# Second layer of a two-layer encoder: how the positional part of the latent heads is rotated and multiplied, and one block of values placed earlier

## The chip, the cores and the metric

One core of a Trainium2 chip runs the whole kernel. The metric is the device time of one execution in microseconds (us); lower is better. The engines that matter are TensorE (PE, matrix products, with its weight loads PEld), VectorE (DVE), ScalarE (ACT), GpSimd (POOL), and SyncE (SP), which issues nearly all DMA transfers. Each engine takes its own instructions in the order in which they were written to its queue.

## The reference, cut to what matters

Two layers; in each, two groups of attention heads read one input projection, and a dense MLP follows. The change touches the second group, multi-head latent attention. The sequence has 256 tokens, and there are 8 latent heads. A head's scores are a sum of a content part (128 features) and a positional part (64 features, rotated by the token's position); the positional key is shared by all heads.

```python
def _rope(x, cos, sin):
    half = x.shape[-1] // 2
    x1, x2 = x[..., :half], x[..., half:]
    out = jnp.concatenate([x1 * cos - x2 * sin, x2 * cos + x1 * sin], axis=-1)
    return out.astype(x.dtype)

# latent attention, per block of queries
s = (jnp.einsum('bhqd,bhkd->bhqk', qn, knt)
     + jnp.einsum('bhqr,bkr->bhqk', qr, k_rope)).astype(jnp.float32) * scale
p = jax.nn.softmax(s, axis=-1)
return jnp.einsum('bhqk,bhkd->bhqd', p.astype(vt.dtype), vt)

# where its inputs come from, in layer l
q = (_rmsnorm(cq, q_norm_g[l]) @ w_uq[l]).reshape(B, S, MLA_HEADS, MLA_NOPE + MLA_ROPE)
q_nope = q[..., :MLA_NOPE]
q_rope = _rope(q[..., MLA_NOPE:], cos[:, :, None, :], sin[:, :, None, :])
kv = (_rmsnorm(ckv, kv_norm_g[l]) @ w_ukv[l]).reshape(B, S, MLA_HEADS, MLA_NOPE + MLA_V)
k_nope, v_m = kv[..., :MLA_NOPE], kv[..., MLA_NOPE:]
k_rope = _rope(kr, cos, sin)
```

All data is float32.

## The kernel before, in words

**Split products.** Most products are not done in fp32. Both operands are split into a high part `hi`, the value rounded to the type fp32r, and a low part `lo`, the rest; then hi x hi, hi x lo and lo x hi are added up in PSUM (`mac`, lines L194, L197 and L198; for values with tokens as rows `tokens_by_k`, L296 to L298). Weights come from memory as fp32 blocks of 128x2048 (1 MB, tile `raw`, 5 buffers), and each half of a block is converted by ACT (`hi`, L151) and DVE (`lo`, L154) into one of 4 buffers each. Some products take fp32 operands as they are: scores, transposes, and the products of probabilities and values. In the trace an fp32 product appears as two records, one of fp32r operands as one.

**Stages of the second layer's attention.** First the projections: the compressed queries `cq`, the compressed keys and values `ckv`, then the queries, keys and the positional key of the input projection. `keys` makes the positional key (`rope_k`). `col` and `probs` make the keys and the probabilities of the 4 differential heads, `turn` transposes those. Then come small up-projections, each of one block of weights: `up_k` (keys of the 8 latent heads, tiles `kn`), `up_q(0)` and `up_q(1)` (content queries, `qn`), `up_r` (positional queries, `qr`) and `up_v` (latent values, `vm`, in banks `pv`). `val(cg, kq)` are 8 blocks of the differential heads' values, 24 products each; the four blocks of a group add up in two PSUM banks (`pv`), which they hold until the fourth has been done.

**A latent head** is three steps from `mla_steps`: `scores` (products into a bank `psm`, one row half of 128 tokens after the other, then a softmax on DVE and ACT), `turn` (a transpose, tile `pt`, copied by ACT to `aT`), and `values` (bank `pom`). The list `mla` holds the steps of all 8 heads staggered: scores of one head, the transpose of the one before, the values of the one before that. Its first six steps stand between the up-projections; the remaining 18 and two steps of the differential heads are handed to `interleave`, which puts them between the blocks of `val`.

**The positional part.** A tile `qr` has 128 rows: 64 features of one head and 64 of the next, for two such pairs. Rotation needs each group of 32 rows exchanged with its neighbour. `rope_q` does that by a product with a permutation matrix (line L1222, bank `pqr`), then three DVE steps with `cos` and `sin` (L1225 to L1227). The key `kr` has two versions, one with the key in rows 0 to 63 and zeros below (set by POOL) and one the other way round, so that a product over all 128 rows picks out one of the two heads (L1319); L1318 is the content product.

**What sets the order.** A scheduler puts each engine's instructions in line by their dependences and by its own estimate of when they become ready; the order of the calls in `layer` breaks ties. PSUM has 8 banks of 2 KB per row. Between the blocks the columns of `w_ada`, the modulation's weights, are loaded (tile `ada`) and summed on DVE (L380), a number per block set by `rate`.

Of the kernel before, what the change touches and what calls it, by code (L numbers as in the profile page):

```python
# [9 lines left out]
F32 = mybir.dt.float32  # L10
F32R = mybir.dt.float32r
I32 = mybir.dt.int32
AF = mybir.ActivationFunctionType
ALU = mybir.AluOpType
AX = mybir.AxisListType

P = 128
T = 256
# [4 lines left out]
HM = 8  # L23
# [78 lines left out]
class Trunk:  # L102
# [764 lines left out]
    def layer(self, l, acc=None):  # L867
        nc, io = self.nc, self.io
        qs = 1.0 / math.sqrt(128.0)
        ms = 1.0 / math.sqrt(192.0)  # L870
# [29 lines left out]
        cq, ckv = [], []  # L900
        kk, qn, kn, qr, vm, a, at, v, o = [], [], [], [], [], [], [], [], []
        self.mo = []

        def keys():
            ps = self.bank("pkr")
            self.tile_cols(ps[:, 0], io["w_kr"][l], h)
            self.kr = self.rope_k(ps[:, 0])

        def col(i, out, scale):
            def f():  # L910
# [7 lines left out]
        def up_k():  # L918
            kn.extend(self.copy(ps, "kn") for ps in self.small(io["w_uk"][l], ckv, 8))
# [2 lines left out]
            qn.extend(self.copy(ps, "qn", ms) for ps in self.small(io["w_uq"][l, b], cq, 4))  # L922

        def up_r():
            raw = [self.copy(ps, "qr", ms) for ps in self.small(io["w_uq"][l, 2], cq, 4)]
            qr.extend(self.rope_q(x) for x in raw)

        def up_v():
            w = self.weights(io["w_uv"][l])
# [5 lines left out]
        def val(cg, kq):  # L935
            def f():
                if kq == 0:
                    self.pv = [self.bank("pv") for _ in range(2)]
                w = self.weights(io["w_dv"][l, cg, kq])
                w = [[z[:, 512 * j : 512 * j + 512] for z in y] for y in w for j in range(2)]  # L940
                self.tokens_by_k(self.pv, w, h[4 * kq : 4 * kq + 4], kq == 0, kq == 3)
                if kq == 3:
                    v.append([self.copy(ps, "v").rearrange("p a b -> p (a b)") for ps in self.pv])
            return f

        def probs(hd):
            return lambda: a.append(self.diff_probs(l, hd, q[hd], kk[hd]))

        def turn(hd):
            return lambda: at.append(self.transposed(a[hd]))  # L950

        av = [self.diff_steps(l, hd, at, v, o) for hd in range(HD)]
        heads = [self.mla_steps(hm, qn, qr, kn, vm) for hm in range(HM)]
        mla = []
        for i in range(HM + 2):
            for s in range(3):
# [9 lines left out]
        kk.append(self.copy(later[0], "k", -1.0))  # L966
        q.append(self.copy(later[1], "q", qs))
        keys()
        order = [(0, kk, -1.0), (2, kk, -1.0), (4, kk, -1.0)]
        for n, (i, dst, scale) in enumerate(order):  # L970
# [4 lines left out]
            col(i + 1, dst, scale)()  # L975
        if l:
            self.rate = RATE_A2
        up_k()
        probs(3)()
        if l == 0:  # L980
# [2 lines left out]
                nc.sync.dma_start(self.xr[:, t], io["x"][t])  # L983
        up_q(0)
        turn(0)()
        up_r()
        turn(1)()
        mla[0]()
        up_v()
# [7 lines left out]
        if l == 0:  # L997
            self.rate = RATE_V
        self.interleave(
            [val(cg, kq) for cg in range(2) for kq in range(4)],  # L1000
            mla[6:] + [av[0][0], av[1][0]],
        )
        if l == 0:
# [9 lines left out]
        o = self.mo + o  # L1013
# [11 lines left out]
        for fb in range(NFB):  # L1025
            hid = []
            done = 12 - 6 * l
            for m in range(0 if fb else done, NK, 2):
                srcs = [io[f"w_m1{l}"][NK * fb + m + j - done] for j in range(2)]
                ps = self.wides(srcs, h)  # L1030
# [197 lines left out]
        return raw  # L1228


    def softmax_parts(self, s, least):

        nc = self.nc
        tot, r = self.s("tot"), self.s("r")
        for t in range(2):
            nc.scalar.activation(
                s[:, t], s[:, t], AF.Exp, bias=least[:, t : t + 1], scale=-1.0, accum_out=tot[:, t : t + 1]
            )
        nc.vector.reciprocal(r, tot)
        return r  # L1240
# [65 lines left out]

        return values, turn

    def mla_steps(self, hm, qn, qr, kn, vm):
        nc = self.nc  # L1310
        st = {}

        def scores():
            ps = self.bank("psm")
            s, mx = self.t("sm"), self.s("mxm")
            for t in range(2):
                c = slice(t * P, (t + 1) * P)
                nc.tensor.matmul(ps[:, t], qn[hm // 2][:, hm % 2, c], kn[hm // 2][:, hm % 2], start=True, stop=False)  # L1318
                nc.tensor.matmul(ps[:, t], qr[hm // 4][:, (hm // 2) % 2, c], self.kr[:, hm % 2], start=False, stop=True)  # L1319
            for t in range(2):  # L1320
                nc.vector.tensor_scalar(s[:, t], ps[:, t], -1.0, None, ALU.mult, ALU.min, accum_out=mx[:, t : t + 1])
            r = self.softmax_parts(s, mx)
            for t in range(2):
                nc.scalar.activation(s[:, t], s[:, t], AF.Copy, scale=r[:, t : t + 1])
            st["s"] = s

        def turn():
            st["t"] = self.transposed(st["s"])

        def values():  # L1330
            if hm % 2 == 0:
                self.pom = self.bank("pom")
            for kt in range(2):
                c = (hm % 4) * P
                v = vm[hm // 4][kt].rearrange("p a b -> p (a b)")
                nc.tensor.matmul(self.pom[:, hm % 2], v[:, c : c + P], st["t"][:, kt], start=kt == 0, stop=kt == 1)
            if hm % 2:
                self.mo += self.split(self.pom, "mo", True)

        return scores, turn, values  # L1340


# [91 lines left out]
```

## Time and profile before

| | |
|---|---|
| median of 3 runs | 2174.59 us (2174.57 to 2177.94) |
| profiled execution, its time | 2174.76 us |
| profiled execution, its span in the trace | 2172.8 us |
| granted TensorE clock, mean | 0.994 |
| second layer's small up-projections start | about 1257 us into the span |
| its last block of values ends | about 1359 us |
| memory read | 589.66 MB, 273 GB/s over the span |

The span is the time from the first to the last instruction in the trace; the device time is some 2 us longer. In the page's rows, "busy" is the time in which an engine has an instruction under way. The chain that ended last is a sequence of pieces of work, each of which released the next; what is not on it costs nothing by itself. A row of a group of instructions reads: line, engine, operation, output<-input, shape, count, then total busy us and mean ns, then the idle time of the engine before it and what ended that. PEclk is the granted clock of TensorE as a share of full speed. A fence of the profile below holds rows word for word; a line of "..." stands for rows left out.

### The profile page before, as it was taken

How to read it: one execution, taken by the hardware profiler on the slowest of the kernel's cores; microseconds unless marked ns; L12 is line 12 of the kernel's file. 1: busy time of each engine (PE TensorE's matmuls, PEld its weight loads, DVE VectorE, ACT ScalarE, POOL GpSimd, SP SyncE). 2: the span in 40 equal slices, each digit the busy share in tenths (PEclk: the TensorE clock that was granted, in tenths of full speed). 3: DMA queues.
4: the chain of work that ended last, by engine and by line, in shares of the span. 5: the costliest groups of instructions: out<-in, count | busy, mean ns of one | idle time of the engine just before them, and what ended most of it. 6: DMA issues, size and time to landing. Idle time of an engine off the chain costs nothing.

```text
span 2172.8 us, 29358 instructions
## 1 busy us (share of the span) xinstructions
PE 2144.7 (99%) x11502; PEld 1863.5 (86%) x11502; DVE 1590.9 (73%) x2117; ACT 1139.8 (52%) x1725; POOL 6.8 (0%) x19
## 2 busy tenths in 40 slices
PE   7999999999999999999999999999999999999998
PEld 6899888898888888888889998888888888888886
DVE  7888888988688988888876876678555555555555
ACT  6555663565455355355454565556535534644643
POOL 0000000000000000000000000000000000000000
PEclk8999999999999999999999999999999999999999
DMA  9988889799888988888967766767655555565552
GB/s 387 423 340 330 320 328 357 290 330 344 314 329 326 352 315 320 321 333 320 336 224 278 253 229 224 290 214 273 233 199 182 200 194 177 192 208 179 194 195 96
DMA packets 87243, 594.76 MB, mean 274 GB/s; under 512 B 9856, under 2 KB 10304, under 8 KB 20288
## 3 DMA queue, kind: packets, MB, share of 16 engines
q1 hardware_dynamic: 85968, 587.08, 73.5%
q0 software_dynamic: 848, 5.28, 0.6%
q8 instruction: 90, 1.47, 0.3%
q10 hardware_dynamic: 288, 0.52, 0.1%
q14 instruction: 49, 0.40, 0.1%
HBM read 589.66 MB, written 3.18 MB: 273 GB/s over the span
## 4 chain that ended last, share of the span: by engine, by line
PE 97%; DVE 2%; DMA 1%; ACT 0%; SPq 0%; issue 0%; ACTq 0%
PE ps L217 19%; PE pr L312 13%; PE pr L311 13%; PE pr L314 13%; PE ps L220 10%; PE pk L260 3%; PE pk L284 2%; PE pk L194 2%; PE pk L198 2%; PE pk L197 2%; PE pv L298 2%; PE pv L296 2%; PE pv L297 2%; PE pk L281 1%; PE ps L198 1%; PE ps L197 1%
## 5 line engine op out<-in xcount | busy, mean ns | idle before, releaser
L154 DVE TENSOR_TENSOR lo<-raw,hi 128x1024 fp32r<-128x1024 f32 (+1 forms) x714 | 836.0, 1194 | 446.2 <-issue 215.5
L151 ACT ACTIVATE hi<-raw 128x1024 fp32r<-128x1024 f32 (+1 forms) x714 | 732.5, 1036 | 694.0 <-PE pr L312 375.9
L380 DVE SCALAR_TENSOR_TENSOR ada<-ada,cond 128x2048 f32<-128x2048 f32 x192 | 438.0, 2285 | 12.0 <-DMA ada<-in_w_ada 11.4
L217 PE MATMUL ps<-h,hi 128*128 128x512 f32 x1856 | 431.5, 390 | 0.0
L217 PEld LDWEIGHTS ps<-h,hi 128*128 128x128 f32 x1856 | 345.2, 188 | 69.4
L311 PE MATMUL pr<-hi,hid 128*128 128x512 f32 x1024 | 398.6, 389 | 0.0
L312 PE MATMUL pr<-hi,hid 128*128 128x512 f32 x1024 | 398.5, 389 | 0.0
L314 PE MATMUL pr<-lo,hid 128*128 128x512 f32 x1024 | 253.5, 389 | 0.0
L220 PEld LDWEIGHTS ps<-h,lo 128*128 128x128 f32 x1856 | 230.3, 192 | 4.5
L220 PE MATMUL ps<-h,lo 128*128 128x256 f32 x1856 | 231.7, 283 | 0.0
L314 PEld LDWEIGHTS pr<-lo,hid 128*128 128x128 f32 x1024 | 192.2, 188 | 39.9
L312 PEld LDWEIGHTS pr<-hi,hid 128*128 128x128 f32 x1024 | 192.3, 188 | 39.7
L311 PEld LDWEIGHTS pr<-hi,hid 128*128 128x128 f32 x1024 | 192.2, 188 | 39.6
L1192 ACT ACTIVATE sum<-ps 128x256 f32<-128x256 f32 x110 | 42.1, 382 | 117.8 <-PE ps L220 117.7
L194 PE MATMUL pk<-h,hi 128*128 128x256 f32 x320 | 90.5, 285 | 0.2 <-ACT h L705 0.2
L198 PE MATMUL pk<-h,lo 128*128 128x256 f32 x320 | 90.5, 283 | 0.0
L197 PE MATMUL pk<-h,hi 128*128 128x256 f32 x320 | 90.5, 283 | 0.0
L260 PE MATMUL pk<-hf,w 128*128 128x256 f32 x384 | 84.1, 379 | 0.5 <-ACT hf L677 0.5
L188 DVE TENSOR_TENSOR hid<-relu,hid 128x256 fp32r<-128x256 f32 x128 | 48.3, 421 | 49.5 <-ACT hid L187 49.5
L260 PEld LDWEIGHTS pk<-hf,w 128*128 128x128 f32 x384 | 72.7, 190 | 10.7 <-ACT hf L677 0.9
L194 PEld LDWEIGHTS pk<-h,hi 128*128 128x128 f32 x320 | 61.1, 192 | 0.6 <-ACT h L705 0.5
L198 PEld LDWEIGHTS pk<-h,lo 128*128 128x128 f32 x320 | 61.3, 192 | 0.2 <-DVE lo L154 0.2
(237 smaller groups left out, 2456.1 us busy)
## 6 DMA issues: line engine op xcount, KB each, us to landing
raw<-in_w_m SPq DMA_DIRECT2D x238, 1024.0 KB, 5.2
ada<-in_w_ada SPq DMA_DIRECT2D x192, 1024.0 KB, 6.5
raw<-in_w_o SPq DMA_DIRECT2D x32, 1024.0 KB, 6.0
raw<-in_w_m SPq DMA_DIRECT2D x24, 768.0 KB, 5.7
raw<-in_w_dv SPq DMA_DIRECT2D x16, 1024.0 KB, 5.5
raw<-in_w_t SPq DMA_DIRECT2D x12, 1024.0 KB, 5.2
w<-in_w_a SPq DMA_DIRECT2D x24, 384.0 KB, 13.5
raw<-in_w_a SPq DMA_DIRECT2D x12, 768.0 KB, 5.4
```

Of the source, the lines that this page charges most:

```text
L151: ins = self.nc.scalar.activation(hi, v, AF.Copy)
L154: ins = self.nc.vector.tensor_tensor(lo, v, hi.bitcast(F32), ALU.subtract)
L194: ins = mm(ps, hi, x[0], start=first, stop=False, skip_group_check=shared)
L197: mm(ps, hi, x[1], start=False, stop=False, skip_group_check=shared)
L198: self.last_mac = mm(ps, lo, x[0], start=False, stop=last, skip_group_check=shared)
L217: mm(ps.rearrange("p a b -> p (a b)"), part(w, k, 0), x[2], start=k == 0, stop=False)
L220: mm(ps[:, 0], part(w, k, 1), x[0], start=False, stop=k == nk - 1)
L260: self.nc.tensor.matmul(ps, v, whole[k], start=first, stop=last, skip_group_check=True)
L311: mm(ps, xh[:, c], part(i, 0), start=kq == 0 and i == 0, stop=False)
L312: mm(ps, xl[:, c], part(i, 0), start=False, stop=False)
L314: self.last_mm = mm(ps, xh[:, c], part(i, 1), start=False, stop=kq == 3 and i == 3)
L380: ins = nc.vector.scalar_tensor_tensor(w, w, 1.0, self.cond, ALU.mult, ALU.mult, accum_out=acc[:, i : i + 1])
```

## The change

It is made in the second layer alone (`l` is 1), but for one detail.

- **Rotation by moved copies.** `rope_q_parts` takes the place of the permutation product: ACT copies the up-projection's bank to `qr` as before, and copies it a second time to `qrr` in four pieces of 32 rows, each to the neighbouring 32 rows. DVE then does the three steps on tiles in SBUF.
- **Split form on 128 rows.** For each head a tile `qrs` is made whose rows hold the high part of its 64 rotated features (a cast on ACT) and, in the other 64 rows, the low part (a subtraction on DVE). The key is split likewise (`rope_k_parts`): its two versions are now the high part and the low part, each repeated in both row halves; the zeros set by POOL go. A head's row half then takes two fp32r products in place of one fp32 product.
- **Order.** `up_r` is called ahead of `up_k` and no longer after the first `turn`; in its place stands the first block of values, `val(0, 0)`. `interleave` gets the remaining 7 blocks for the same 20 steps.
- **In both layers** the second row half of a head now begins with its positional product; in the first layer the products themselves are as before.

```diff
-            self.kr = self.rope_k(ps[:, 0])
+            self.kr = (self.rope_k_parts if l else self.rope_k)(ps[:, 0])
...
         def up_r():
+            if l:
+                qr.extend(self.rope_q_parts(ps, ms) for ps in self.small(io["w_uq"][l, 2], cq, 4))
+                return
             raw = [self.copy(ps, "qr", ms) for ps in self.small(io["w_uq"][l, 2], cq, 4)]
-            qr.extend(self.rope_q(x) for x in raw)
+            qr.extend([self.rope_q(x)] * 2 for x in raw)
...
+        vals = [val(cg, kq) for cg in range(2) for kq in range(4)]
+        if l:
+            up_r()
         up_k()
         probs(3)()
...
         up_q(0)
         turn(0)()
-        up_r()
+        if l == 0:
+            up_r()
+        else:
+            vals.pop(0)()
         turn(1)()
         mla[0]()
...
         self.interleave(
-            [val(cg, kq) for cg in range(2) for kq in range(4)],
+            vals,
             mla[6:] + [av[0][0], av[1][0]],
         )
...
+    def rope_k_parts(self, ps):
+        nc = self.nc
+        t = self.t("krt")
+        for i in range(2):
+            s = slice(64 * i, 64 * i + 64)
+            nc.vector.tensor_tensor(t[s, 0], ps[:64], self.cos[:64], ALU.mult)
+            nc.vector.tensor_tensor(t[s, 1], ps[64:], self.sin[:64], ALU.mult)
+        both = self.t("krb")[:, 0]
+        for i in range(2):
+            s = slice(64 * i, 64 * i + 64)
+            nc.vector.tensor_tensor(both[s], t[s, 0], t[s, 1], ALU.add)
+        out = self.u("kr", F32R)
+        nc.scalar.activation(out[:, 0], both, AF.Copy)
+        nc.vector.tensor_tensor(out[:, 1], both, out[:, 0].bitcast(F32), ALU.subtract)
+        return out
+
+    def rope_q_parts(self, ps, scale):
+        nc = self.nc
+        raw = self.copy(ps, "qr", scale)
+        rot = self.t("qrr")
+        for i in range(4):
+            j = i ^ 1
+            nc.scalar.activation(rot[32 * i : 32 * i + 32], ps[32 * j : 32 * j + 32], AF.Copy, scale=scale)
+        wide = lambda x: x.unsqueeze(1).broadcast_to([P, 2, T])
+        nc.vector.tensor_tensor(rot, rot, wide(self.sin), ALU.mult)
+        nc.vector.tensor_tensor(raw, raw, wide(self.cos), ALU.mult)
+        nc.vector.tensor_tensor(raw, raw, rot, ALU.add)
+        out = []
+        for i in range(2):
+            both = self.u("qrs", F32R)
+            s, o = (slice(64 * j, 64 * j + 64) for j in (i, 1 - i))
+            nc.scalar.activation(both[s], raw[s], AF.Copy)
+            nc.vector.tensor_tensor(both[o], raw[s], both[s].bitcast(F32), ALU.subtract)
+            out.append(both)
+        return out
...
-                nc.tensor.matmul(ps[:, t], qn[hm // 2][:, hm % 2, c], kn[hm // 2][:, hm % 2], start=True, stop=False)
-                nc.tensor.matmul(ps[:, t], qr[hm // 4][:, (hm // 2) % 2, c], self.kr[:, hm % 2], start=False, stop=True)
+                rope = qr[hm // 4][hm % 2][:, (hm // 2) % 2, c]
+                if l:
+                    steps = [(rope, self.kr[:, 0]), (rope, self.kr[:, 1])]
+                else:
+                    steps = [(rope, self.kr[:, hm % 2])]
+                steps.insert(len(steps) * t, (qn[hm // 2][:, hm % 2, c], kn[hm // 2][:, hm % 2]))
+                for i, (w, x) in enumerate(steps):
+                    nc.tensor.matmul(ps[:, t], w, x, start=i == 0, stop=i == len(steps) - 1)
```

How the engines' instructions stand now, at three places of the second layer. A row is a line of the kernel, an operation, its output tile <- its input tiles, and a shape; the numbers behind names tell tiles apart. The changed kernel's lines are its own (L1315 is the transpose, L1372 every product of a head's scores, L1283 the softmax's exponential).

PE, from the end of the up-projection of positional queries to the first latent head's scores, before (`pt` is the transpose of a differential head, `pv` the banks of the latent values):

```order
L1222 MATMUL pqr_11496<-qr_11467,K 128x512
L1222 MATMUL pqr_11502<-qr_11494,K 128x512
L1268 MATMUL pt_11508<-ident,a_11032 128x128 x4
L1318 MATMUL psm_11515<-kn_11277,qn_11392 128x256
L296 MATMUL pv_11542<-hi_11533,lath_10685 128x512
L297 MATMUL pv_11542<-lo_11534,lath_10685 128x512
L298 MATMUL pv_11542<-hi_11533,latl_10686 128x512
L296 MATMUL pv_11543<-hi_11533,lath_10685 128x512
L297 MATMUL pv_11543<-lo_11534,lath_10685 128x512
L298 MATMUL pv_11543<-hi_11533,latl_10686 128x512
L296 MATMUL pv_11542<-hi_11537,lath_10685 128x512
L1319 MATMUL psm_11515<-kr_10759,qr_11467 128x256
```

And now, from the end of the first block of values (these `pv` are the differential heads' banks):

```order
L297 MATMUL pv_11527<-lo_11535,h_9829 128x512
L298 MATMUL pv_11527<-hi_11534,h_9829 128x512
L1315 MATMUL pt_11563<-ident,a_11034 128x128 x4
L1372 MATMUL psm_11570<-kn_11373,qn_11490 128x256
L1372 MATMUL psm_11570<-kr_10762,qrs_11301 128x256 x4
L1372 MATMUL psm_11570<-kn_11373,qn_11490 128x256
L296 MATMUL pv_11600<-hi_11590,lath_10685 128x512
```

The two permutation products are gone, a block of values stands ahead of the first head, and the head's scores now stand in one piece.

ACT, from the copy of the last differential key (`k`) on, before:

```order
L346 ACTIVATE k_11251<-ps_11099 128x512
L346 ACTIVATE kn_11277<-pss_11264 128x512
L346 ACTIVATE kn_11292<-pss_11279 128x512
L346 ACTIVATE kn_11307<-pss_11294 128x512
L151 ACTIVATE hi_11430<-raw_11428 128x1024
L346 ACTIVATE kn_11322<-pss_11309 128x512
L151 ACTIVATE hi_11434<-raw_11428 128x1024
L1236 ACTIVATE s_11325,tot_11331<-s_11325,mx_11326 128x256 x2
```

And now:

```order
L346 ACTIVATE k_11253<-ps_11101 128x512
L346 ACTIVATE qr_11291<-pss_11266 128x512
L1264 ACTIVATE qrr_11293<-pss_11266 32x512 x4
L151 ACTIVATE hi_11453<-raw_11451 128x1024
L151 ACTIVATE hi_11457<-raw_11451 128x1024
L1273 ACTIVATE qrs_11301<-qr_11291 64x512
L1273 ACTIVATE qrs_11304<-qr_11291 64x512
L346 ACTIVATE qr_11332<-pss_11307 128x512
L1264 ACTIVATE qrr_11334<-pss_11307 32x512 x4
L151 ACTIVATE hi_11530<-raw_11528 128x1024
L151 ACTIVATE hi_11534<-raw_11528 128x1024
L1283 ACTIVATE s_11421,tot_11427<-s_11421,mx_11422 128x256
```

The copies of positional queries, the moved copies and the casts have come in ahead of the copies of keys (`kn`).

SP, the loads of weights for this stretch, before:

```order
L170 DMA raw_11253<-in_w_uk 128x2048
L170 DMA raw_11355<-in_w_uq 128x2048
L364 DMA ada_11365<-in_w_ada 128x2048
L170 DMA raw_11428<-in_w_uq 128x2048
L364 DMA ada_11440<-in_w_ada 128x2048
L170 DMA raw_11531<-in_w_uv 128x2048
L170 DMA raw_11608<-in_w_uq 128x2048
```

And now:

```order
L170 DMA raw_11255<-in_w_uq 128x2048
L170 DMA raw_11348<-in_w_uk 128x2048
L364 DMA ada_11358<-in_w_ada 128x2048
L170 DMA raw_11451<-in_w_uq 128x2048
L364 DMA ada_11463<-in_w_ada 128x2048
L170 DMA raw_11528<-in_w_dv 128x2048
L170 DMA raw_11588<-in_w_uv 128x2048
```

The block of the positional queries has moved ahead of the keys' block, and a block of values (`w_dv`) ahead of the latent values' (`w_uv`).

More of the change, by code (lines that the diff above doesn't have):

```diff
@@ L952, in layer @@
         av = [self.diff_steps(l, hd, at, v, o) for hd in range(HD)]
-        heads = [self.mla_steps(hm, qn, qr, kn, vm) for hm in range(HM)]
+        heads = [self.mla_steps(l, hm, qn, qr, kn, vm) for hm in range(HM)]
         mla = []
@@ L1307, in diff_steps, with mla_steps @@
         return values, turn
-    def mla_steps(self, hm, qn, qr, kn, vm):
+    def mla_steps(self, l, hm, qn, qr, kn, vm):
         nc = self.nc
```

## The prediction

> **What bounds the kernel now.** I read the page's parts 1 and 4 first (busy shares, and the chain that ended last), then the busy time by stretch around the second layer's latent heads, the chain of that stretch piece by piece, and last the queues of ACT and DVE there.
>
> ```profile
> PE 2144.7 (99%) x11502; PEld 1863.5 (86%) x11502; DVE 1590.9 (73%) x2117; ACT 1139.8 (52%) x1725; POOL 6.8 (0%) x19
> ...
> PE 97%; DVE 2%; DMA 1%; ACT 0%; SPq 0%; issue 0%; ACTq 0%
> ```
>
> TensorE (PE) is busy for 99% of the span and makes 97% of the chain. But a share over the whole span proves nothing for one stage, so here are six stretches of the second layer (columns: stretch, its length, then busy us of PE, PEld, DVE, ACT and POOL, the granted clock, the DMA share and GB/s).
>
> ```profile
> 1257.20:1263.10 5.90, 5.90 (x51) 5.90 (x50) 2.60 (x5) 3.52 (x6) 0.00 (x0) 1.00 0.80 285
> 1263.10:1270.60 7.50, 7.50 (x59) 7.29 (x58) 6.60 (x17) 5.06 (x12) 0.00 (x0) 1.00 0.43 149
> 1270.60:1276.80 6.20, 6.20 (x55) 6.20 (x54) 5.60 (x7) 4.08 (x7) 0.00 (x0) 1.00 0.76 244
> 1276.80:1278.75 1.95, 1.95 (x7) 0.61 (x6) 1.60 (x4) 1.87 (x3) 0.00 (x0) 1.00 1.00 424
> 1278.75:1289.00 10.25, 10.25 (x54) 8.72 (x52) 5.66 (x13) 6.32 (x14) 0.00 (x0) 1.00 0.56 208
> 1289.00:1352.00 63.00, 63.00 (x321) 53.99 (x320) 41.47 (x73) 37.58 (x77) 0.00 (x0) 1.00 0.65 228
> ```
>
> In all six PE's busy time equals the length, at full clock. Busy PE may still be waiting inside modelled ends, so the chain of the same stretch (start, length, piece) is the better witness:
>
> ```profile
> 1263.27 1.73 PE psc L1249 x8
> ...
> 1273.93 0.12 PE pss L198
> 1274.05 0.12 PE pss L194
> ...
> 1276.93 1.97 PE pqr L1222 x4
> 1278.90 0.44 PE pt L1268 x4
> 1279.34 0.43 PE psm L1318 x2
> 1279.77 0.23 PE pv L296
> ...
> 1281.40 0.43 PE psm L1319 x2
> ```
>
> Each piece starts where the one before ends, and all are PE's. So here a microsecond of PE work is a microsecond of the kernel. The rows also give the prices. An fp32 product 128x256 is two records ("x2") and takes 0.43 us; a product of two fp32r operands of the same size is one record and takes 0.12 us. Going from one kind to the other costs nothing: eight fp32 records, amid fp32r work, take 1.73 us, and 4 x 0.43 is 1.72.
>
> **The change, part by part.**
>
> *The permutation products (L1222) go.* Two fp32 products with 512 columns, 1.97 us in the chain. Their own share is about 1.73 (twice the columns of L1249's, half the count); the rest is a wait for ACT's second copy, since the product needs the copied tile:
>
> ```profile
> PEld pqr L1222 <- ACT qr L346: 0.8, 1, 0.8
> ```
>
> Both vanish, the wait because a block of values (24 products of 0.23 us, 5.5 us) now stands between the last up-projection and the first head. Gain 1.97.
>
> *The positional scores.* Each of 8 heads has two row halves. Before, a half had one fp32 rope product, 0.43; now it has two fp32r products, 2 x 0.12 = 0.24. 16 x (0.43 - 0.24) = 3.04 us. That 0.12 holds for these products too is read from L194 to L198, which have the same 128x128 weights, 128x256 movers and fp32r types. Bounds: at L1319's pace per record (0.215) the gain would be nil; at that of the cheapest record in the chain, a transpose of 128 columns (0.44 for four, 0.11 each), it would be 16 x 0.21 = 3.4. The row of the same form decides: 0.12.
> [...]
>
> *The moved copies and split tiles, on ACT and DVE.* The nearest rows:
>
> ```profile
> L572 ACT ACTIVATE bias<-pb 32x512 f32<-32x512 f32 x16 | 9.4, 587 | 0.8 <-PE pb L569 0.7
> L182 ACT ACTIVATE lath<-lt 128x512 fp32r<-128x512 f32 x6 | 3.7, 623 | 4.7 <-DVE lt L725 4.7
> L1226 DVE TENSOR_TENSOR qr<-qr,cos x2: 681/683/685, 1279.0 to 1280.8; 128x512 f32<-128x512 f32 x2
> L187 ACT ACTIVATE mo<-pom 128x256 fp32r<-128x256 f32 x16 | 6.0, 377 | 7.5 <-PE pom L1336 3.9 <-DVE mo L188 3.6
> L1215 DVE TENSOR_TENSOR kr<-krt 64x256 f32<-64x256 f32 x4 | 1.7, 420 | 0.1
> ```
>
> ACT gains eight 32-row copies (8 x 0.59 = 4.7 us; L572 has just this form and also moves rows), four 64-row casts (4 x 0.62 = 2.5) and the key's cast (0.4): 7.6 us. DVE keeps six rotation steps and adds four subtractions (4 x 0.68 = 2.7) and one for the key (0.4). None is on PE, so they cost nothing as long as what PE takes from these two queues comes in time. From 1257 to 1289 ACT was busy for 20.9 of 31.8 us and DVE for 22.1, so the room is there; but both serve in order, and that needs a walk.
>
> The rows that fix the walk (columns: start, length, engine, line, tile):
>
> ```profile
> 1258.45 0.58 ACT L346 ACTIVATE k<-ps 128x512 f32<-128x512 f32 x1
> ...
> 1260.42 0.60 ACT L346 ACTIVATE kn<-pss 128x512 f32<-128x512 f32 x1 [0.84 <-PE pss L198]
> ...
> 1269.99 1.06 ACT L151 ACTIVATE hi<-raw 128x1024 fp32r<-128x1024 f32 x1 [1.39 <-issue]
> 1270.96 1.07 ACT L346 ACTIVATE qn<-pss 128x512 f32<-128x512 f32 x2
> ```
>
> PE, without waits, from 1257.3 (48 products of 0.12 ahead of 1263.1, where the table's second stretch begins): rotary queries (48 products of 0.12) to 1263.0, keys to 1268.8, scores of the fourth differential head to 1270.5, queries to 1276.3, a transpose of 0.44, the values to 1282.2, a transpose, and head 0 at 1282.6. ACT: the first pair of columns can be copied at 1260.4, as the second pair of keys was; the four moved copies end at about 1262.9, two conversions (hi) at 1264.8, the casts at 1265.8, the second pair's copies at 1268.2, two conversions at 1270.7, then a softmax step that waits for DVE (1272.4), two casts (1273.4), four key copies (1275.3), uv's conversions and softmax steps (1279.1), and a conversion for the next queries, which waits until PE has used half the block of values (1280.6). Behind it stands the copy qn that head 0 needs: ready at 1281.1, wanted at 1282.6. That 1.5 us is the thinnest cover; DVE's low parts (lo) of each block come 2 to 3 us early. Four banks of keys are copied out by 1275.3, before the transpose and the values ask for banks at 1276.3 to 1276.9.
>
> *The key's split (rope_k_parts)* puts a cast on ACT that waits for DVE's rotated key, in front of a square of cq; then on DVE a subtraction. The reciprocal of cq's norm moves from 1224.43 to about 1224.7, and PE's spread wants it at 1225.27:
>
> ```profile
> 1224.43 0.16 DVE L649 RECIPROCAL rms<-rms 128x2 f32<-128x2 f32 x1
> ...
> 1225.27 0.61 PE L651 MATMUL pn<-ident,rms 128*128 128x128 f32 x4
> ```
>
> Cover about half a microsecond, cost nil. The removed POOL memset (0.5 us) was on no path.
>
> *Moved loads on SP.* uq's third block goes ahead of uk, the first values ahead of uv; as many loads as before. A load of 1 MB lands after 5.5 us; that block of values was issued at 1270.00 and first converted at 1287.59:
>
> ```profile
> raw<-in_w_dv SPq DMA_DIRECT2D x16, 1024.0 KB, 5.5
> ...
> 1270.00 0.33 SPq L170 DMA_DIRECT2D raw<-in_w_dv  x1
> ...
> 1287.59 2.01 ACT L151 ACTIVATE hi<-raw 128x1024 fp32r<-128x1024 f32 x2
> ```
>
> Twelve microseconds of cover; cost nil. *Seven blocks instead of eight between the later heads*: a head's transpose now comes 8.1 us after its scores (block 5.5, another head's values 0.87, scores 1.34, a transpose 0.44). The slowest softmax that I found there ends 5.8 us after the start of its last score product:
>
> ```profile
> 1297.55 0.87 PE pom L1336 x4
> ...
> 1322.01 0.59 PE L1319 MATMUL psm<-kr,qr 128*128 128x256 f32 x2
> ...
> 1326.90 0.89 ACT L1324 ACTIVATE sm<-sm,r 128x256 f32<-128x256 f32 x2
> ```
>
> So nil. *First layer*: in each head's second half the rope product now precedes the other; same products, nil.
>
> **Sum.** 1.97 + 3.04 = 5.0 us off PE. The profiled run took 2174.76 (span 2172.8 and 1.96 around it), so 2169.75; the median of the runs, 2174.59, lies 0.17 lower. I forecast 2169.6.
>
> **Rivals.** The bound that a measurement of this kernel can tell from no change is 0.2%, 4.35 us, so 0.66 us of new waiting already turns my gain into "no change".
>
> *A wait takes the gain back (ACT in order).* The row at 1270.96 shows two copies of query columns that ran 3 us after the first was ready (its 24 products end 2.9 us after the piece of 1263.27, at 1267.9), behind a conversion that waited for a weight buffer. Now casts that wait for DVE join that queue. If it is 3 us later than my walk, head 0 waits 1.5 us: 2171.1; should it slip at several heads, up to the full 5: 2174.6. For it: the thin 1.5 us. Against: the queue idles at 1268 to 1270 now, and lateness does not add up there.
> [...]
>
> *Slower: banks.* The two banks of values are now held from 1276.7 until the fourth block, some 40 us, beside up-projections and heads that request about 19 banks from the six left. If six were too few, each request would wait for an ACT copy, 0.6 us: 19 x 0.6 = 11.4, less 5.0, gives 2181. It decides from 0.5 us per request on. Against it: from 1289 to 1352 the values already hold two banks, and PE shows 63.00 busy of 63.00.
>
> *It does not do what it says.* If split products ran at 0.215 each, only 1.97 is gained: 2172.8.
>
> **How the numbers follow.** Forecast (new waits under 0.66 us): 0.68. ACT's queue, with waits from 0.66 to 5 us: 0.22. The slow split: 0.05. Banks: 0.05. Faster 0.68; within 0.2% 0.22 + 0.05 = 0.27; slower 0.05. The range runs from 2169.0 (0.11 per split product gives 2169.2, and the runs and the profiled one differ by 0.2) to 2172.8 (the slow split, or 3 us of waits), leaving out about 1 in 10 above and less below.
>
> **What would show it.** Right: no L1222 piece for layer two, a head's scores of 1.34 us in the chain instead of 1.73, PE busy for the whole stretch. Wrong: a wait of PE for ACT's qn, for a vm or aT copy (banks) or for the cast tiles; or rope products at 0.2 us in the chain.

## The result and the profile after

The changed kernel took 2169.38 us (median of 7 runs, 2167.3 to 2170.03), the kernel before 2174.59 beside it (7 runs, 2173.38 to 2177.94): a ratio of 0.9973 with a 95% interval of 0.9964 to 0.9983, formed from all these runs (the two medians alone give 0.9976). A second measurement, eleven runs beside the experiments, gave 0.9977 (0.9968 to 0.9986). Forecast were 2169.6 us, a ratio of 0.9977. So the change makes the kernel faster by a quarter of a per cent, between 5 and 6 us.

Busy time and the engines' shares of the chain, from the page of the changed kernel:

```profile
PE 2140.6 (99%) x11498; PEld 1861.7 (86%) x11498; DVE 1593.9 (74%) x2122; ACT 1148.1 (53%) x1738; POOL 6.3 (0%) x18
...
PE 96%; DVE 2%; DMA 1%; ACT 1%; SPq 0%; issue 0%; ACTq 0%
```

TensorE's busy time fell by 4.1 us and the span by 5.2 (2172.8 to 2167.6); ACT's busy time rose by 8.3, DVE's by 3.0. To place the gain I cut out one stage of the second layer, from TensorE's spread of `cq`'s norm (L651, tile `pn`) to the first product of the differential heads' values (tile `po`). Busy time in just that stage (columns as in the table of stretches in the prediction), before:

```profile
1225.27:1359.37 134.10, 134.10 (x821) 120.40 (x820) 95.89 (x183) 81.27 (x158) 0.00 (x0) 1.00 0.66 233
```

and after:

```profile
1225.39:1354.22 128.83, 128.83 (x817) 117.45 (x816) 98.75 (x187) 88.14 (x170) 0.00 (x0) 1.00 0.70 247
```

The stage is 5.27 us shorter, and all of that is TensorE's; everything outside it together took as long as before (2038.7 and 2038.8 us). Over the whole span TensorE's busy time fell by only 4.1 us, because outside the stage it was busy for 1.2 us more (2011.8 against 2010.6) in a time of the same length. Within the stage TensorE is busy all the time, at full clock: four more DVE and twelve more ACT instructions lengthened nothing.

The chain of the changed kernel around the first two heads and the third:

```profile
1282.54 0.44 PE pt L1315 x4
1282.98 1.34 PE psm L1372 x8
1284.32 0.23 PE pv L296
...
1290.22 1.34 PE psm L1372 x8
...
1298.19 1.33 PE psm L1372 x8
```

A head's scores, still eight records, take 1.34 us where four pairs of 0.43 (1.73) stood. No piece of `pqr` is left in this layer. 8 x (1.73 - 1.335) = 3.16 and 1.97 make 5.13 of the 5.27.

ACT's queue of the changed kernel, which I had walked through ahead (a bracket gives the idle time before a row and what ended it; from 1258 to 1273 us its rows start in the order in which the program queued them):

```profile
1260.54 0.60 ACT L346 ACTIVATE qr<-pss 128x512 f32<-128x512 f32 x1 [1.39 <-PE pss L198]
1261.16 2.40 ACT L1264 ACTIVATE qrr<-pss 32x512 f32<-32x512 f32 x4
1263.59 2.01 ACT L151 ACTIVATE hi<-raw 128x1024 fp32r<-128x1024 f32 x2
1265.50 1.27 ACT L1273 ACTIVATE qrs<-qr 64x512 fp32r<-64x512 f32 x2
...
1279.09 2.00 ACT L151 ACTIVATE hi<-raw 128x1024 fp32r<-128x1024 f32 x2
1280.99 1.05 ACT L346 ACTIVATE qn<-pss 128x512 f32<-128x512 f32 x2
```

Four moved copies in 2.40 us are 0.60 each, where 0.59 was priced. The first `qn` copy is done at about 1281.5, and the transpose ahead of head 0 ends at 1282.98: 1.5 us of cover (the time by which a result is ready before it is wanted), the figure of the prediction.

### The profile page after: what moved, and what is told of

Read it like the earlier page. It is cut to its first block, busy times and chain, and to the rows that moved or that the text cites. A ratio compares the mean times of both kernels' runs of the same rounds, so it can differ in the third digit from the quotient of the medians.

```text
span 2167.6 us, 29372 instructions
## 1 busy us (share of the span) xinstructions
PE 2140.6 (99%) x11498; PEld 1861.7 (86%) x11498; DVE 1593.9 (74%) x2122; ACT 1148.1 (53%) x1738; POOL 6.3 (0%) x18
## 4 chain that ended last, share of the span: by engine, by line
PE 96%; DVE 2%; DMA 1%; ACT 1%; SPq 0%; issue 0%; ACTq 0%
PE ps L217 19%; PE pr L311 13%; PE pr L312 13%; PE pr L314 13%; PE ps L220 10%; PE pk L260 3%; PE pk L284 2%; PE pk L194 2%; PE pk L198 2%; PE pk L197 2%; PE pv L296 2%; PE pv L298 2%; PE pv L297 2%; PE psm L1372 1%; PE pk L281 1%; PE ps L197 1%
```

## The experiments

All are variants of the changed kernel in which four things are set for each layer apart, in the order (first, second): MOVED (rotation by moved copies), SPLIT (split scores), RFIRST (`up_r` ahead of `up_k`) and AHEAD (blocks of values ahead of the first latent head). Their line numbers are one to eight higher than the changed kernel's. The change is `(0, 1)` in all four. A ratio is to the kernel before on the same chip; a stage is read from one trace of each kernel.

### Taking the change apart

**The change itself**, once more, with the three below on the same chip:

```diff
+MOVED, SPLIT, RFIRST, AHEAD = (0, 1), (0, 1), (0, 1), (0, 1)
```

> The changed kernel again, beside the kernel before on one chip. Stage meant in all runs: from PE's spread of cq's norm in the second layer to the first product of a differential head's values; 134.10 us before, 128.83 in the first trace after. Theory 'PE work': all of the gain is PE work taken out of that stage, 1.97 us of permutation products and their wait and 3.2 us of scores, so the stage is 128.8 again and the ratio 0.9976, within 0.0005. Rival 'something more': the ratio of 0.9973 of the first seven runs means that another 0.7 us went elsewhere; then the ratio is 0.9973 or less and a second stage of the trace is shorter.

2170.01 us, ratio 0.9977 (0.9968 to 0.9986). The stage:

```profile
1225.37:1354.23 128.86, 128.86 (x818) 117.43 (x816) 98.74 (x187) 88.14 (x170) 0.00 (x0) 1.00 0.68 246
```

The stage is the same again to 0.03 us, and the ratio is that of the stage's 5.2 us. So nothing supports the rival that another 0.7 us went elsewhere, though the interval of the time alone does not rule it out.

**The order alone**:

```diff
-MOVED, SPLIT, RFIRST, AHEAD = (0, 1), (0, 1), (0, 1), (0, 1)
+MOVED, SPLIT, RFIRST, AHEAD = (0, 0), (0, 0), (0, 1), (0, 1)
```

> The order alone: in the second layer the positional queries' up-projection stands ahead of the keys' and one block of values ahead of the first latent head, but rotation is by the permutation product and the scores are fp32 as before. 'PE work': only the wait in front of the second permutation product (0.25 us) can go, stage 133.8 to 134.1, ratio 0.9998 to 1.0000. Rival 'order': the block of values covers waits that the change as a whole would otherwise show, and brings most of the gain by itself; stage 131 or less, ratio 0.9986 or less.

2175.19 us, ratio 1.0001 (0.9992 to 1.0009). The stage, then the permutation products in the chain, then the wait of their weight loads (total, times, longest):

```profile
1226.34:1360.35 134.01, 134.01 (x822) 120.38 (x821) 95.98 (x183) 81.21 (x158) 0.00 (x0) 1.00 0.65 236
```

```profile
1264.33 1.97 PE pqr L1233 x4
```

```profile
PEld pqr L1233 <- ACT qr L347: 0.8, 1, 0.8
```

The order gains 0.1 us, so the rival that it brings most of the gain is out. The products cost 1.97 and show the wait of their loads as before, though a block of values now stands behind them.

**Order and moved copies, scores in fp32**:

```diff
-MOVED, SPLIT, RFIRST, AHEAD = (0, 1), (0, 1), (0, 1), (0, 1)
+MOVED, SPLIT, RFIRST, AHEAD = (0, 1), (0, 0), (0, 1), (0, 1)
```

> The new order and rotation by moved copies, but no split: scores by fp32 products with the zero-padded key. 'PE work': 1.97 us less, stage 132.1, ratio 0.9991. Rival 'copies on ACT cost': ACT's queue gets the moved copies (4.8 us) and returns them as waits of PE; stage 134 or more.

2173.13 us, ratio 0.9990 (0.9981 to 0.9999). The stage:

```profile
1225.88:1357.92 132.04, 132.04 (x818) 119.74 (x817) 95.97 (x183) 85.50 (x166) 0.00 (x0) 1.00 0.66 240
```

**Order and split scores, rotation by permutation products**:

```diff
-MOVED, SPLIT, RFIRST, AHEAD = (0, 1), (0, 1), (0, 1), (0, 1)
+MOVED, SPLIT, RFIRST, AHEAD = (0, 0), (0, 1), (0, 1), (0, 1)
```

> The new order and the split scores, but rotation by the permutation product. 'PE work': 8 heads at 1.34 instead of 1.73 us, 3.2 us less and at most 0.25 of a wait, stage 130.7 to 131.0, ratio 0.9985. Rival 'the split needs the copies': casts behind the permutation product and its three DVE steps come too late for the first head; stage 132 or more.

2172.01 us, ratio 0.9987 (0.9978 to 0.9996). The stage:

```profile
1224.53:1355.35 130.82, 130.82 (x822) 118.09 (x821) 98.41 (x187) 83.60 (x162) 0.00 (x0) 1.00 0.68 243
```

Against the order alone, the copies take 134.01 - 132.04 = 1.97 us off the stage, the split 134.01 - 130.82 = 3.19, both together 5.15: a sum of 5.16. The parts add up, as they must where TensorE is never kept waiting, and neither the copies nor the casts cost it a wait.

### Is there a cover, and how thick?

**Without the block of values ahead**:

```diff
-MOVED, SPLIT, RFIRST, AHEAD = (0, 1), (0, 1), (0, 1), (0, 1)
+MOVED, SPLIT, RFIRST, AHEAD = (0, 1), (0, 1), (0, 1), (0, 0)
```

> The change without the block of values ahead of the first latent head: all eight blocks stand between the later heads, the products are the same. Cover theory: head 0 then wants the query copy at about 1277.3 us, 5.5 us earlier, while ACT still has its queue to work off and brings it at about 1280.5: a new wait of some 3 us, about 2173. Rival, no cover needed (ACT finds room, as it had in the kernel before with a wait of 0.25): no wait, 2170.0. Bank rival: the values' banks are held for a shorter time, so the kernel is faster than with the block.

2174.22 us, ratio 0.9998 (0.9990 to 1.0007): by the times nearly the whole gain is gone. The only wait of TensorE in the stage, and the chain there:

```profile
PE psm L1379 <- ACT qn L347: 3.2, 1, 3.2
```

```profile
1280.69 0.95 ACT hi L152
1281.64 0.49 ACT qn L347
...
1282.17 1.60 PE psm L1379 x8
```

Head 0 stands for 3.2 us behind ACT's `qn`, and its scores then take 1.60 us in place of 1.34. The stage took 132.30 us, 3.44 more than the change's, which is those two. That is still 1.8 less than before, so by the stage two thirds of the gain are gone and not all of it; the interval of the ratio holds both. So the block is what gives ACT the time for its longer queue: the new order as a whole is worth 0.1 us by itself, and the block alone is worth 3.4 once the copies and casts are there.

**Each moved copy twice** (the second writes the same values again):

```diff
             j = i ^ 1
-            nc.scalar.activation(rot[32 * i : 32 * i + 32], ps[32 * j : 32 * j + 32], AF.Copy, scale=scale)
+            for _ in range(2):
+                nc.scalar.activation(rot[32 * i : 32 * i + 32], ps[32 * j : 32 * j + 32], AF.Copy, scale=scale)
```

> The change with each moved copy of 32 rows issued twice (the second writes the same values again): eight more ACT instructions of 0.60 us, 4.8 us in ACT's queue ahead of the query copy, TensorE's work unchanged. ACT-in-order theory: the copy was ready 1.8 us before head 0 wanted it and ACT's queue had only 0.8 us of idle time in that stretch, so head 0 waits some 2.5 to 3 us: about 2172.8. Rival, ACT has slack enough anyway: no wait, 2170.0.

2174.98 us, ratio 1.0001 (0.9992 to 1.0010). 4.8 us more on ACT lengthened the stage by 5.51, twice what I expected. TensorE's waits in it:

```profile
PE pt L1323 <- ACT qrr L1267: 2.0, 1, 2.0
PE pss L195 <- DVE mx L1306: 1.5, 1, 1.5
```

and the stretches around the first of them (the granted clock is the third number from the right):

```profile
1281.00:1282.00 1.00, 0.39 (x4) 0.40 (x5) 1.00 (x1) 0.97 (x3) 0.00 (x0) 1.00 1.02 426
1282.00:1283.00 1.00, 1.00 (x6) 0.86 (x5) 1.00 (x4) 1.00 (x5) 0.00 (x0) 0.69 1.03 385
1283.00:1284.00 1.00, 1.00 (x4) 0.71 (x4) 1.00 (x3) 1.00 (x2) 0.00 (x0) 0.50 0.98 393
1284.00:1285.00 1.00, 1.00 (x4) 0.81 (x3) 0.97 (x2) 0.95 (x3) 0.00 (x0) 0.50 0.24 98
1285.00:1286.00 1.00, 1.00 (x5) 0.76 (x4) 0.97 (x2) 1.00 (x3) 0.00 (x0) 0.61 0.46 90
1286.00:1287.00 1.00, 1.00 (x6) 0.83 (x5) 0.97 (x4) 1.00 (x3) 0.00 (x0) 1.00 0.66 147
```

The direction is that of ACT in order, but not the place: the scheduler set other steps between the copies, so the late work hit an up-projection and a transpose, not head 0. Neither of the two reads what it waited for: the transpose reads `a`, and the step named beside it copies a bank `pss` to `qrr`; the up-projection waits for a maximum of a softmax, taken from a bank `psc`. So these are most likely waits for a PSUM bank that is read out late; this is argued from the operands, no run tests it. The 3.5 us of waiting explain two thirds of the 5.5. The granted clock of the four rows from 1282 to 1286 us (0.69, 0.50, 0.50, 0.61) falls 1.7 us short of full speed, as much as 3.4 us at half would, so some 1.7 us of work are lost; together 5.2. Here 3.5 us of waiting made the stage 5.5 us longer, so work that comes late can cost more than its lateness.

**Two blocks ahead**:

```diff
-MOVED, SPLIT, RFIRST, AHEAD = (0, 1), (0, 1), (0, 1), (0, 1)
+MOVED, SPLIT, RFIRST, AHEAD = (0, 1), (0, 1), (0, 1), (0, 2)
```

> The change with two blocks of values ahead of the first latent head instead of one; six stand between the later heads. Cover theory: one block already covers ACT's queue (head 0 had no wait), the second adds nothing: 2170.0. Bank rival: the values' two banks are held for 5.5 us longer beside the heads and up-projections, and the wait for banks shows as PE waiting for copies of vm, aT or pss: 2172 or more. Softmax rival: with six blocks for twenty steps some heads stand without a block in between, and a transpose waits for a softmax of 5.8 us: 2172 to 2176.

2169.50 us, ratio 0.9976 (0.9967 to 0.9985). The stage:

```profile
1226.30:1355.17 128.87, 128.87 (x817) 117.45 (x816) 98.87 (x187) 88.71 (x170) 0.00 (x0) 1.00 0.69 248
```

To a hundredth the change's own. The values' banks are held for another 5.5 us, six blocks stand between the heads, and TensorE never waits: neither the banks nor the softmax hold it up here.

### The same in the first layer

There the stage from the first `pn` spread to the first `po` product took 151.41 us in the kernel with the change; TensorE was busy for 147.61 of them, part of that at a lowered clock.

**Everything in both layers**:

```diff
-MOVED, SPLIT, RFIRST, AHEAD = (0, 1), (0, 1), (0, 1), (0, 1)
+MOVED, SPLIT, RFIRST, AHEAD = (1, 1), (1, 1), (1, 1), (1, 1)
```

> The whole change in the first layer too. Work theory: the same 5.2 us of TensorE work goes there (1.97 for the permutation products, 3.2 for the scores), so about 2164.8 us against 2170.0 for the change, if DVE and ACT have room. DVE theory: in the first layer's small up-projections (208 to 224 us) TensorE already waits for converted weights and DVE is nearly always busy, so the 3.1 us of new DVE work lengthen that wait: about 2168. Room theory: the block of values put ahead gives the converters 5.5 us, so the 2.3 us wait near 213 us and the stretch of lowered granted clock behind it (0.74 from 215.4 to 222 us) go as well: 2160 to 2162.

2169.64 us, ratio 0.9982 (0.9973 to 0.9992): no gain over the change, and none of the three expected times. The first layer's stage took 149.89 us, of which TensorE was busy for 142.63: 5 us less work, but 3.5 us more waiting. Nearly all of the waiting is one wait:

```profile
PE pss L195 <- ACT hi L152: 7.0, 1, 7.0
```

ACT's queue ahead of it:

```profile
200.40 2.40 ACT L1266 ACTIVATE qrr<-pss 32x512 f32<-32x512 f32 x4
205.84 1.28 ACT L1280 ACTIVATE qrs<-qr 64x512 fp32r<-64x512 f32 x2 [3.05 <-DVE qr L1270]
...
216.04 2.94 ACT L152 ACTIVATE hi<-raw 128x1024 fp32r<-128x1024 f32 x3
```

and DVE's, where the rotation stands behind a sum of the modulation:

```profile
201.58 2.29 DVE L381 SCALAR_TENSOR_TENSOR ada<-ada,cond 128x2048 f32<-128x2048 f32 x1
...
203.79 0.69 DVE L1268 TENSOR_TENSOR qrr<-qrr,sin 128x512 f32<-128x512 f32 x1
```

This looks like the rival that I had priced for the second layer: a cast waits for DVE, and the conversions that TensorE needs wait behind the cast. The 3.05 us for which ACT stood idle ahead of that cast, with the conversions of 216.04 still to come, agree. But that idle time is not what makes the difference: the last kernel of this section has it too (3.04 us).

**A block ahead in the first layer, nothing else there**:

```diff
-MOVED, SPLIT, RFIRST, AHEAD = (0, 1), (0, 1), (0, 1), (0, 1)
+MOVED, SPLIT, RFIRST, AHEAD = (0, 1), (0, 1), (0, 1), (1, 1)
```

> The change, and in the first layer one block of values ahead of its first latent head, with that layer's rotation and order of up-projections as before. Cover theory: the first layer's wait of 2 us behind two conversions at about 221.7 us (and its share of the wait at the permutation product) lies under the block: 2 us faster than the change, about 2168. Rival: the wait near 213 us and the lowered clock behind it stand ahead of that block and stay, and the block's own conversions come earlier in the same queues: no gain, 2170.

2170.37 us, ratio 0.9982 (0.9974 to 0.9991), the stage 152.34 us: no gain. The block by itself is worth nothing there.

**Split scores there, nothing else**:

```diff
-MOVED, SPLIT, RFIRST, AHEAD = (0, 1), (0, 1), (0, 1), (0, 1)
+MOVED, SPLIT, RFIRST, AHEAD = (0, 1), (1, 1), (0, 1), (0, 1)
```

> The change, and in the first layer the split scores alone (permutation products, order and blocks there as before). Work theory: 3.2 us less TensorE work in the first layer, 2166.8. In-order rival: DVE has no idle time from 226 to 236 us there and ACT idles for DVE; casts and subtractions (2.5 and 2.7 us) come between the rotation and head 0, which now waits for 1.3 + 1.4 us or more: 2168.5 to 2171.

2173.15 us, ratio 0.9991 (0.9983 to 1.0000), the stage 152.67 us, 1.3 longer than the change's. A new wait of TensorE, the longest:

```profile
PE pt L1322 <- ACT sm L1384: 2.7, 1, 2.7
```

Behind that wait the granted clock fell again:

```profile
237.00:241.50 4.50, 4.18 (x23) 4.18 (x24) 4.50 (x7) 3.98 (x10) 0.00 (x0) 0.62 0.48 146
```

The 3.2 us of scores are gone and more than paid back, by the 2.7 us of waiting and some 1.7 us of work lost to the clock (0.38 of 4.5 us). The casts and subtractions stand ahead of the softmax in the queues of ACT and DVE; that they are what put it off is argued from this order. Expected was a wait at head 0; it came one step later, and the time lies above both expectations.

**Split scores and a block ahead there**:

```diff
-MOVED, SPLIT, RFIRST, AHEAD = (0, 1), (0, 1), (0, 1), (0, 1)
+MOVED, SPLIT, RFIRST, AHEAD = (0, 1), (1, 1), (0, 1), (1, 1)
```

> As the one before, with one block of values ahead of the first latent head in the first layer too. Cover theory: the block's 5.5 us cover the casts and subtractions, so the full 3.2 us show: 2166.8 to 2167.2. In-order rival: the block's own conversions, two on ACT and two on DVE, go into the same queues ahead of the rotation: no better than 2169.

2169.50 us, ratio 0.9976 (0.9967 to 0.9985); the stage 149.08 us, 2.3 shorter than the change's. In place of the wait of 2.7 us stands a shorter one, at a head's scores:

```profile
PE psm L1379 <- DVE sm L1381: 1.1, 1, 1.1
```

The block covers most, not all, and the time is the rival's (no better than 2169).

**And the positional queries first there**:

```diff
-MOVED, SPLIT, RFIRST, AHEAD = (0, 1), (0, 1), (0, 1), (0, 1)
+MOVED, SPLIT, RFIRST, AHEAD = (0, 1), (1, 1), (1, 1), (1, 1)
```

> As the one before, with the first layer's positional queries ahead of its keys, as in the second layer (its rotation still by permutation products). If the first layer's loss in the kernel with everything in both layers came from the moved copies (4.8 us of ACT), this order is free of it and gives 2166.8 or less. If it came from the early place (casts on ACT that wait for a rotation on DVE behind a sum of 2.3 us, ahead of the conversions that TensorE needs next), the wait of several us stays: 2170 or more.

2165.86 us (6 runs, 2164.76 to 2171.7), ratio 0.9967 (0.9955 to 0.9979): the fastest of all that ran. The first layer's stage and TensorE's waits there:

```profile
154.10:299.89 145.79, 142.47 (x904) 128.54 (x903) 129.38 (x229) 87.65 (x170) 0.00 (x0) 1.00 0.86 320
```

```profile
PE pss L195 <- ACT hi L152: 1.8, 1, 1.8
PE pss L199 <- DVE lo L155: 1.2, 1, 1.2
```

The stage is 5.6 us shorter than with the change: 3.2 from the scores, and most of the rest because the clock stays at 1.00, where with the change it fell (1.7 us of work, from the stretches in the last section; TensorE waits for 3.3 us in place of 3.8). The kernel differs from the one with everything in both layers in the first layer's moved copies alone, so those were what broke that one. The cast's wait for DVE is not the difference, for here too ACT idles for 3 us ahead of the casts:

```profile
206.87 2.61 ACT L1280 ACTIVATE qrs<-qr 64x512 fp32r<-64x512 f32 x4 [3.04 <-DVE qr L1238]
```

Without the eight copies (4.8 us) in the same queue TensorE's wait for the conversions is 1.8 us and not 7.0. In that stretch two permutation products on TensorE (1.8 us in the chain) are cheaper than eight copies on ACT. The kernel's interval still overlaps that of the change (0.9968 to 0.9986, on another chip), so its lead of 0.1% is shown by the stage and made likely, not settled, by the times.

## What the prediction had right, and the step that failed

**The bound.** "In all six PE's busy time equals the length": right, and it carried everything. With it, work off TensorE is time off the kernel, and the parts measured one by one add up to within 0.01 us.

**Permutation products, 1.97.** Right in size (1.97 measured). The reason that I gave for its last quarter was wrong: the block of values does not remove the wait for ACT's second copy. In the kernel with the order alone the products keep the same wait and still cost 1.97. It goes because the products go.

**Scores, 3.04.** Too small: 3.16 from the chain, 3.19 from the pair of experiments. Rounded rows are why: eight fp32 records measure 1.73, so an fp32 product takes 0.4325 and not 0.43; eight records of mixed kinds measure 1.335, so a split product takes 0.1175 and not 0.12; 16 of the one and 32 of the other add up to the 0.12 us that two decimals hide. With the 0.1 us of the order, which the sum put at nothing, the 5.0 us of the sum are 5.27 in the stage.

**The covers.** ACT ran up to 1.6 us behind my walk in the middle (the second pair's copies end at 1269.8, not 1268.2) and 0.4 at its end; the 1.5 us of cover were there. In the stage ACT gained 6.9 us (predicted for the twelve instructions in it 7.2) and DVE 2.9 (2.7 for its four). The key's split moved the reciprocal of `cq`'s norm, and TensorE took its result without a wait:

```profile
1224.79 0.16 DVE L649 RECIPROCAL rms<-rms 128x2 f32<-128x2 f32 x1
...
1225.39 0.61 PE L651 MATMUL pn<-ident,rms 128*128 128x128 f32 x4
```

I had said 1224.7. Loads and the seven blocks between the later heads cost nothing, as forecast, and neither did the reordered products of the first layer (its stage took 151.48 us before and 151.41 with the change).

**The rivals.** Banks as priced (six left of the eight tiles in the kernel's pool `pp`), a wait at each request: ruled out, TensorE is busy all through the stage, and with two blocks ahead as well. The slow split: ruled out by 1.34 us a head. ACT in order: it did not happen here, but it was the right thing to fear. Without the block it takes 3.4 us of the stage's gain back; with 4.8 us more on ACT, all of it; and in the first layer, with the moved copies, the stage gained 1.5 us where 5.2 us of work went. For this rival I had read the wait of 3 us in the kernel before as one for a weight buffer; the row itself names no releaser ("issue"), so what that conversion waited for is not shown.

**What failed: the low end of the range.** The measured median, 2169.38, lies 0.2 us below the forecast. But the first ratio, 0.9973, put on the median of 2174.59 makes 2168.7, below my 2169.0. The step that failed is the one that built this end: it took one term, the price of a split product (0.11 in place of 0.12), and 0.2 us from "the runs and the profiled one differ by 0.2". The scatter of the measurement itself it put at nothing. What the runs showed in its place: the seven of the changed kernel spread over 2.7 us, and the interval of the first ratio, 0.9964 to 0.9983, is 2166.8 to 2170.9 us, some 2 us each way. The three runs I had been shown, 2174.57 to 2177.94, could have told me. The sum was short too, but that alone would have stayed inside: the stage's 5.27 us off 2174.59 make 2169.3. The other 0.6 us down to 2168.7 stand in no stage (everything outside took 2038.7 and 2038.8 us) and did not come again in the second measurement; as far as is known they are scatter. That the second ratio, put on 2174.59, gives the forecast of 2169.6 to the tenth is luck: its interval is 4 us wide, and the sum was 0.26 short.

## What to carry to other kernels

Where one engine is busy without a gap, the price of its instructions from the chain gives the gain of removing them (here 5.0 us forecast, 5.27 measured in the stage); the risk lies in what the work moves to, so walk that engine's queue in order and find the thinnest cover. The range of a forecast needs the scatter of the runs on both sides as well as the errors of its terms. A reordering that is worth nothing by itself (0.1 us here) can be what makes another change pay (3.4 us): test it with the change, not alone. The same edit can gain in one layer (5.2 us of the second layer's stage) and bring next to nothing in another (1.5 us of the first's, and none in the time), where the queue that takes the work is already late for something that is needed.

## What was not expected of the hardware

The granted clock fell to half after some of TensorE's waits: 0.50 in the stretch from 1283 to 1285 us after the wait of 2.0 us in the kernel with doubled copies, and likewise in the first layer of the kernel with the change (behind its wait of 2.1 us near 213 us), where products of 0.12 us took 0.21. Stretches there, in the run beside the experiments:

```profile
215.00:216.00 1.00, 0.56 (x4) 0.34 (x3) 1.00 (x2) 0.71 (x1) 0.00 (x0) 0.86 0.32 131
216.00:217.00 1.00, 0.93 (x4) 0.93 (x5) 1.00 (x2) 0.00 (x0) 0.00 (x0) 0.50 0.06 25
217.00:218.00 1.00, 1.00 (x7) 1.00 (x6) 1.00 (x2) 0.00 (x0) 0.00 (x0) 0.50 0.00 0
218.00:219.00 1.00, 1.00 (x6) 1.00 (x6) 1.00 (x1) 0.00 (x0) 0.00 (x0) 0.50 0.90 164
219.00:220.00 1.00, 1.00 (x9) 1.00 (x9) 1.00 (x3) 0.00 (x0) 0.00 (x0) 0.94 0.81 336
220.00:221.00 1.00, 1.00 (x11) 1.00 (x10) 1.00 (x1) 0.18 (x1) 0.00 (x0) 1.00 1.01 426
```

The rows from 215 to 220 us fall 1.70 us short of full speed, which makes 3.4 us at half; those of the doubled copies above make the same. In the kernel before, behind a wait of 2.1 us too, it was 6.8 us (0.60 in the microsecond from 214, 0.50 in the six after it, 0.99 in the next). In the kernel with everything in both layers it began within the wait of 7.0 us, and a mean clock of 0.86 over 7 us and of 0.51 over 5 us makes 6.9 us at half:

```profile
210.00:217.00 7.00, 0.12 (x1) 0.00 (x0) 4.33 (x15) 6.54 (x17) 0.00 (x0) 0.86 0.21 88
217.00:222.00 5.00, 4.84 (x21) 4.44 (x22) 5.00 (x6) 2.93 (x4) 0.00 (x0) 0.51 0.17 23
```

Length of wait alone does not decide it: 3.2 us without the block ahead brought no drop (the clock was 1.00 in every stretch from 1274 to 1300 us), two waits of 1.8 and 1.2 us in the fastest kernel's first layer none either (1.00 from 198 to 226 us), while waits of 2.0 and 2.1 us did. What decides it, and how long the clock stays at half, is open here.
